# Emptying the seventh product's bank on ScalarE, and fixed places and a written order for the states of a state-space stage

## The chip, the core and the metric

The kernel runs on one core of a Trainium2 chip. The metric is the device time of one execution, in microseconds (us). Engines are named as in the profile: PE is TensorE (matmuls; PEld is its weight load, which overlaps), DVE is VectorE, ACT is ScalarE, POOL is GpSimd, SP is the queue that issues loads. ACT's queue issues the stores (ACTq in the profile's rows).

## The reference

One layer, model width 1024, sequence 1024, batch 1, float32. Two branches work on the same modulated input `h` and are merged by gates:

```python
proj = h @ w_in
gm_u, gm_v, gm_z, ssm_z, xbc, dt_raw, g_a, g_b = jnp.split(proj, SPLITS, axis=-1)
y_a = spatial_gating(gelu(gm_u), gelu(gm_v), ...) * silu(gm_z)          # 8 groups, chunks of 128
xbc = silu(causal_depthwise_conv(xbc, conv_w, conv_b))                  # 4 taps
xs, bm, cm = jnp.split(xbc, ...)
y_b = ssd_scan(xh, dt, a, bm, cm) + xh * d_skip[:, None]                # 8 groups of 4 heads of 64, state 128
y_b = rms_norm(y_b * silu(ssm_z), ssm_norm_w)                           # over each group
merged = sigmoid(g_a) * (y_a @ w_proj_a) + sigmoid(g_b) * (y_b @ w_proj_b)
out = rms_norm(x + gate * (merged @ w_out), final_norm_w)
```

`ssd_scan` works in chunks of 128. With the running sums `acs` of `dt*a` in a chunk, what a chunk gives is

```python
y_diag = (C_l . B_s) * exp(acs_l - acs_s) [l >= s] @ (x * dt)           # within the chunk
y_off  = (C_l @ state_before) * exp(acs_l)                              # from earlier chunks
state  = state * exp(acs_end) + B^T @ (x * dt * exp(acs_end - acs))     # handed on
```

## The kernel before

Every large product is kept at float32 precision by splitting both factors into a high and a low half (hi = rounded to `fp32r`, the type that PE takes; low = the rest), and adding three products: hi·hi, hi·lo, lo·hi. A rounding cast on ACT makes the high half, a subtraction on DVE the low one. The large products also use Strassen–Winograd: seven block products, `p1` to `p7`, in place of eight.

The order of work is partly written out. `pin` keeps an instruction in program order on its engine (all matmuls and transposes, by `mm` and `tp` at L81 and L84, and all loads, by `load` at L90); the rest is placed by a scheduler, which puts what stands under `high_priority` first. `later(n, f)` puts off a piece of work by n slots; a slot ends with `run_tasks`, after each product or item.

In the order in which PE comes to them:

1. Transposes, modulation and the first gate products (0 to some 70 us). `first_gate` ends with four `sg<-acc` activations on ACT (L473), each reading one PSUM bank.
2. The v block, `v_block` (L860 to L925): 28 units, each one of seven products at one of four `k`. A unit is 12 matmuls into four banks: `vx0` to `vx3`, or `vy0` to `vy3`. For each bank in turn come the three terms (`bh·wh`, `bl·wh`, `bh·wl`), `b` being the activations' halves and `w` the weights' (`p1v0h`, `p1v0l` for the first unit; the low half comes from DVE at L850).
3. The wide stage: pairs of output columns, `pair` (L540 to L598), of `cb`, `x`, `uz`, `z` and `g` columns, the number being the group. Each product is 12 matmuls (L536). `p1`, `p6`, `p7` and `p4` accumulate in one bank, `x…`; `p5` and `p3` in another, `y…`; `p2` in a third. After each product the bank is emptied by an operation under `high_priority`, recorded at L552: ACT copies for `p1`, `p5`, `p6` and `p4`, DVE adds for `p3`, `p2` and `p7`. The add after `p7` is `c2 = p5 + bank`; `p4`, which accumulates on in the same bank, is put off until after the next pair's `p5`, that is two products later. Beside it run the casts of the next pair's weights (L522 on ACT, L523 on DVE), the convolutions, and the splitting of the merged projections' weights (`wba`, `wbb`, `wbc`, from loads `wbr`; L787 on ACT, L792 on DVE, stored by `wb_d`).
4. The state-space stage, some 925 to 1146 us: a list of 32 steps, each a group and a pair of chunks, two groups alternating (`order`). `Group` holds the parts of a step:
   - `fetch`: two loads, `dcy` (running sums, broadcast) and `sl` (C, B, x and z of the two chunks), in a ring of 5 places.
   - `decay`: `ea` (ACT, L1063), the causal `affine_select` of `dcy` (POOL, L1066), eight exponentials on `dcy` (ACT, L1071).
   - `prep`: matmuls and transposes into the banks `pc` (C·B, and B transposed) and `px` (x transposed), then `xd` and `xe` (DVE, L1087), `dcy` times `pc` (DVE, L1091), and `bn`, the copy of B transposed (ACT, L1093).
   - `front`: eight matmuls into `yi` (within the chunks), the matmuls into `sp` (what each chunk adds to the state), and for each chunk a new state `st` in a ring of places: POOL multiplies the last state by its decay (L1119), DVE adds `sp` (L1121); the first one of a group is a DVE copy (L1117).
   - `back`: the matmuls into `yn` (from earlier chunks), then `evacuate`: `y` = d_skip·x + `yi` (DVE, L1147), `ym` = `yn`·`ea` (DVE, L1151), their sum (POOL, L1152), times z (POOL, L1153).
   - `post`: stores, then the squares (ACT, L1172, and a POOL add, L1173) put off by 5 slots, and the sums of squares later.

   Between these items `draw` puts in a few matmul pairs of `proj_a` (`pma`), the product with `w_proj_a`, which is independent of them. Its weights are split by `wa_block` at k = 1 of the block before: `wah` (ACT, L1276) and `wal` (DVE, L1277). For step n the list issues front(n), a draw, back(n), prep(n+2), fetch(n+6), decays(n+4).
5. The merged projections (L1548, 1146 to some 1330 us) and the output products (L1741, to the end).

Of the kernel before, what the change touches and what calls it, by code (L numbers as in the profile page):

```python
# [8 lines left out]
F32 = mybir.dt.float32  # L9
# [26 lines left out]
def hybrid_kernel(  # L36
# [505 lines left out]
    def pair(name, ops, done1, done2, after=None, whole=False):  # L542
# [7 lines left out]
        def out(f, *a):  # L550
            with tc.high_priority():
                keep(f(*a))  # L552
# [258 lines left out]
    def v_block():  # L811
# [94 lines left out]
        for u, (nm, k) in enumerate(units):  # L906
            _, bn, pn = V_OPS[u // 4]
            if u == 4:
                ps["y"] = [bank(f"vy{j}") for j in range(4)]
            for j in range(4):  # L910
                js = slice(j * P, (j + 1) * P)
                (bh, bl), (wh, wl) = (bop[bn][v][k] for v in range(2)), wops[u]
                for n, (l, r) in enumerate(((bh, wh), (bl, wh), (bh, wl))):
                    pin(PE.matmul(ps[pn][j], l[:, js], r, start=nm in ("p1", "p5", "p2") and n + k == 0,  # L914
                                  stop=n == 2 and k == 3, skip_group_check=nm not in ("p1", "p5", "p2")))
# [118 lines left out]
    nstep, nst = [0], [0]  # L1034

    class Group:

# [35 lines left out]
        def prep(self, s):  # L1073
            g, nm = self.g, f"{self.g}_{s}"
            sl, dcy, ea = self.pre[s]
            px, pc = bank(f"px{nm}"), bank(f"pc{nm}")
            for i in range(2):
                tsl = slice(i * P, (i + 1) * P)
                mm(pc[:, i * P : (i + 1) * P], sl[:, 1, tsl], sl[:, 0, tsl])
                tp(pc[:, 256 + i * P : 256 + (i + 1) * P], sl[:, 1, tsl], ident)  # L1080
                tp(px[:, i * 256 : i * 256 + P], sl[:, 2, tsl], ident)
                tp(px[:, i * 256 + P : i * 256 + 256], sl[:, 3, tsl], ident)
            x4 = px.rearrange("p (i h w) -> p i h w", i=2, h=HPG)
            xs = []
            for v, f in (("xd", dthq), ("xe", dde)):
                t = p2x.tile([P, 512], F32, name=f"{v}{nm}", tag=v, bufs=3)
                V.tensor_tensor(t.rearrange("p (i h w) -> p i h w", i=2, h=HPG), x4,  # L1087
                                fac(f, g, s).unsqueeze(3).to_broadcast([P, 2, HPG, HD]), op=ALU.mult)
                xs.append(t)
            d3 = dcy.rearrange("p h i l -> p h (i l)")  # L1090
            V.tensor_tensor(d3, d3, pc[:, 0:256].unsqueeze(1).to_broadcast([P, HPG, 256]), op=ALU.mult)  # L1091
            bn = p2x.tile([P, 256], F32, name=f"bn{nm}", tag="bn", bufs=3)
            A.copy(bn, pc[:, 256:512])  # L1093
            self.pre[s] = (sl, dcy, bn, xs[0], xs[1], ea)

        def front(self, s):
# [11 lines left out]
            self.y[s] = yi  # L1108
            self.sts = [self.st]
            for i in range(2 if s < NCH // 2 - 1 else 1):  # L1110
                mm(sp[:, i * 256 : (i + 1) * 256], bn[:, i * P : (i + 1) * P], xe[:, i * 256 : (i + 1) * 256])
            for i in range(2 if s < NCH // 2 - 1 else 1):
                pool, tag, b = st_r[nst[0] % 4 if nst[0] % 4 < 3 else 2]
                nst[0] += 1
                s2 = pool.tile([P, 512 if pool is hp else 256], F32, name=f"st{nm}_{i}", tag=tag, bufs=b)[:, 0:256]
                if self.st is None:
                    V.tensor_copy(s2, sp[:, 0:256])  # L1117
                else:
                    G.tensor_mul(v3(s2), v3(self.st),  # L1119
                                 fac(cd, g, s)[:, i].unsqueeze(2).to_broadcast([P, HPG, HD]))  # L1120
                    V.tensor_add(s2, s2, sp[:, i * 256 : (i + 1) * 256])  # L1121
                self.st = s2
                self.sts.append(s2)

        def back(self, s):

# [7 lines left out]
            self.evacuate(s, self.y.pop(s), yn)  # L1134
            if s % 2:
                self.post(s // 2)

        def evacuate(self, s, yi, yn):
# [6 lines left out]
            y1 = turn(y1_r, f"y1{nm}", F32).rearrange("p (j t) -> p j t", j=2)  # L1145
            for j in range(2):
                V.scalar_tensor_tensor(y1[:, j], sl[:, 2 + j], dskt[:, 2 * g + j : 2 * g + j + 1],  # L1147
                                       yi[:, j * 256 : (j + 1) * 256], op0=ALU.mult, op1=ALU.add)
            m = turn(ym_r, f"ym{nm}", F32).rearrange("p (j t) -> p j t", j=2)
            t0 = 0 if s else P  # L1150
            V.tensor_tensor(m[:, :, t0:], yn.rearrange("p (j l) -> p j l", j=2)[:, :, t0:], ea[:, :, t0:], op=ALU.mult)  # L1151
            G.tensor_add(y1[:, :, t0:], y1[:, :, t0:], m[:, :, t0:])  # L1152
            G.tensor_mul(yz, y1, sl[:, 4:6])  # L1153

        def post(self, q):

# [102 lines left out]
            pin(V.tensor_sub(yl[i], f32(yl[i]), f32(yh[i])))  # L1259
        yas.append((yh, yl))  # L1260

    war_r, wah_r, wal_r = [], [], []

    def wa_load(dd):
        war[dd] = []
# [6 lines left out]
    def wa_block(dd):  # L1272
        was[dd] = []
        for i, wr in enumerate(war.pop(dd)):
            wh, wl = turn(wah_r[0], f"wah{dd}_{i}"), turn(wal_r[0], f"wal{dd}_{i}")
            A.copy(wh, wr)  # L1276
            V.tensor_sub(wl, wr, f32(wh))  # L1277
            was[dd].append((wh, wl))

    def beside(n):  # L1280
# [74 lines left out]
    def proj_a():  # L1355

        for dd in range(KT):
# [8 lines left out]
            for k in range(KT):  # L1366
# [6 lines left out]
                    yield  # L1373
                if k == 1 and dd + 1 < KT:
                    wa_block(dd + 1)
            keep = pin if dd == KT - 1 else lambda i: i
            for h in range(2):
                keep(V.scalar_tensor_tensor(ths[h], ths[h], 1.0, pms[h], op0=ALU.add, op1=ALU.mult))
# [6 lines left out]
    st_r = [(hp, room.pop(0), 1), (p2x, "st", 1), (p2q, "st", 2)]  # L1385
    fetch(4)
    wa_load(1)
    fetch(5)
# [43 lines left out]
        run_tasks()  # L1432


    room.extend(ea_r[0] + [st_r[0][1]])
    room.extend(tag for k in range(KT - 2) for tag in ya_tags[k])
    draw(left[0] - 5)

# [439 lines left out]
```

## Time and profile before

| what | value |
|---|---|
| runs shown | 1401.98, 1403.64, 1404.79 us |
| median | 1403.64 us |
| the profiled execution | 1405.65 us, its span 1403.9 us, granted clock 0.995 |
| PE busy | 1371.6 us, 98% of the span, 6971 matmuls and transposes |
| DVE busy | 1053.8 us, 75% |
| ACT busy | 787.1 us, 56% |
| POOL busy | 212.4 us, 15%, most of it in the state-space stage |
| moved by DMA | 288.62 MB, 206 GB/s |

The profile records one execution: every instruction with its start, its length and what it waited for. A row of a view of waits reads: engine, what it works on, its line, then who released it; the total in us, how often, and the longest. A row of the timeline reads: start and length in us, engine, line, operation, out<-in, the shapes, and in brackets the idle time ahead of it with its releaser. A row of groups reads: line, engine, operation, shapes, count, then busy us and the mean length in ns, and the idle time ahead.

### The profile page before, as it was taken

What the parts mean: (1) busy time and instruction counts of PE and PEld (TensorE: products, weight loads), DVE (VectorE), ACT (ScalarE), POOL (GpSimd) and SP (SyncE); (2) the same over time, 40 slices, a digit from 0 to 9 for tenths busy, and PEclk for the clock granted to TensorE, in tenths of its full rate; (3) what the DMA queues carried; (4) which work ended last, traced back from release to release, by engine and by line L of the source; (5) the groups of instructions that cost most, each with busy time, mean ns of one, the idle gap of its engine ahead of it and who ended that gap; (6) DMA issues with size and microseconds to landing.
All of it is one profiled execution on the core that took longest, in us unless ns stands there. A gap on an engine that the chain in (4) does not pass through costs nothing.

```text
span 1403.9 us, 20510 instructions
## 1 busy us (share of the span) xinstructions
PE 1371.6 (98%) x6971; PEld 1134.5 (81%) x6971; DVE 1053.8 (75%) x1815; ACT 787.1 (56%) x1459; POOL 212.4 (15%) x208
## 2 busy tenths in 40 slices
PE   8999999999999999999999999999999999999997
PEld 7678888888888788787888888888888887888886
DVE  4777776687777889788888886388767765859976
ACT  5754656656656555455666555587766724223443
POOL 0000000000000011110100010027778750000001
PEclk9999999999999999999999999999999999999999
DMA  8675433343434777777665874498777758978913
GB/s 264 195 240 145 121 118 120 105 123 118 135 105 133 211 211 215 223 240 234 213 196 159 260 222 120 167 349 305 270 260 279 258 188 275 333 254 315 379 45 120
DMA packets 277182, 288.62 MB, mean 206 GB/s; under 512 B 15789, under 2 KB 224085, under 8 KB 277077
## 3 DMA queue, kind: packets, MB, share of 16 engines
q1 hardware_dynamic: 182420, 203.76, 45.8%
q10 hardware_dynamic: 94656, 83.54, 17.9%
q8 instruction: 55, 0.90, 0.3%
q14 instruction: 51, 0.41, 0.1%
HBM read 199.79 MB, written 87.46 MB: 205 GB/s over the span
## 4 chain that ended last, share of the span: by engine, by line
PE 67%; DMA 13%; DVE 9%; ACT 4%; issue 4%; POOL 2%; SPq 2%; ACTq 0%; DVEq 0%; POOLq 0%
PE xuz L536 6%; PE x L1548 6%; PE xcb L536 5%; PE yp L1548 5%; PE xx L536 4%; PE xz L536 4%; DMA wbr<-in_w_proj_b_dram 3%; PE vx L914 3%; PE xg L536 3%; PE yuz L536 3%; PE ycb L536 3%; PE pma L81 2%; PE ox L1741 2%; DMA dcy<-acs_d 2%; PE yx L536 2%
## 5 line engine op out<-in xcount | busy, mean ns | idle before, releaser
L755 POOL TENSOR_TENSOR wog<-wog,gb 128x256 f32<-128x256 f32 x16 | 16.7, 1062 | 625.1 <-DMA wog<-in_w_out_dram 625.1
L1071 ACT ACTIVATE dcy<-dcy,nacs 128x128 f32<-128x128 f32 x256 | 78.6, 389 | 14.7 <-POOL dcy L1066 14.2
L1066 POOL TENSOR_SCALAR_AFFINE_SELECT dcy<-dcy 128x1024 f32<-128x1024 f32 x32 | 35.0, 1093 | 136.8 <-ACT ea L1063 136.8
L986 ACT ACTIVATE ac<-ac 128x1024 f32<-128x1024 f32 x32 | 34.0, 1061 | 30.8 <-DVE ac L984 30.7
L1063 ACT ACTIVATE ea<-dcy 64x512 f32<-64x512 f32 x64 | 40.1, 626 | 13.0 <-DMA dcy<-acs_d 12.5
L81 PE MATMUL pma<-yh,wah 128*128 128x512 f32 x128 | 43.4, 420 | 0.0
L81 PE MATMUL pma<-yh,wal 128*128 128x512 f32 x128 | 42.6, 413 | 0.0
L1486 DVE SCALAR_TENSOR_TENSOR yn<-yn,par,rb 128x512 f32<-128x512 f32 x32 | 23.9, 748 | 24.6 <-DMA yn<-yb_d 24.6
L1091 DVE TENSOR_TENSOR dcy<-dcy,pc 128x1024 f32<-128x1024 f32 x32 | 38.9, 1217 | 4.4 <-PE pc L84 3.8
L1153 POOL TENSOR_TENSOR yz<-y,sl 128x512 f32<-128x512 f32 x32 | 41.4, 1293 | 1.1
L1151 DVE TENSOR_TENSOR ym<-yn,ea 128x512 f32<-128x512 f32 (+1 forms) x32 | 19.9, 623 | 28.5 <-PE yn L81 28.2
L81 PE MATMUL pma<-yl,wah 128*128 128x512 f32 x128 | 40.1, 394 | 0.0
L1152 POOL TENSOR_TENSOR y<-y,ym 128x512 f32<-128x512 f32 (+1 forms) x32 | 36.5, 1142 | 14.5 <-DVE ym L1151 13.7
L81 PEld LDWEIGHTS yn<-sl,st 128*128 128x128 f32 x224 | 30.2, 191 | 9.2 <-issue 2.9
L81 PE MATMUL yi<-dcy,xd 128*64 128x128 f32 x512 | 35.8, 283 | 1.8 <-DVE st L1121 1.8
L81 PE MATMUL yn<-sl,st 128*128 128x128 f32 x224 | 31.1, 276 | 6.0 <-DVE st L1121 6.0
L984 DVE SCALAR_TENSOR_TENSOR ac<-c2x,cwt,ac 128x1023 f32<-128x1023 f32 (+2 forms) x24 | 31.2, 1299 | 5.7 <-ACT ac L982 5.6
L81 PE MATMUL sp<-xe,bn 128*128 128x256 f32 x112 | 32.6, 408 | 2.7 <-DVE ssq L1182 1.5
L984 DVE SCALAR_TENSOR_TENSOR ac<-c2cb,cwt,ac 128x1023 f32<-128x1023 f32 (+2 forms) x24 | 31.1, 1294 | 4.4 <-ACT ac L982 4.3
L1119 POOL TENSOR_TENSOR st<-st,cd 128x256 f32<-128x256 f32 x48 | 32.9, 684 | 7.8 <-PE yn L81 5.5
L1756 POOL TENSOR_TENSOR r<-r,fnw 128x512 f32<-128x512 f32 x2 | 2.5, 1293 | 205.9 <-ACT junk L1754 205.9
L948 ACT ACTIVATE vm<-vm,vr 128x128 f32<-128x128 f32 x64 | 25.8, 484 | 14.0 <-DMA vm<-v_d 13.5
(2903 smaller groups left out, 4402.8 us busy)
## 6 DMA issues: line engine op xcount, KB each, us to landing
sl<-s_d SPq DMA_DIRECT2D x32, 768.0 KB
s_d<-ac ACTq DMA_DIRECT2D x32, 512.0 KB
dcy<-acs_d SPq DMA_DIRECT2D x32, 512.0 KB
av<-in_w_in_dram SPq DMA_DIRECT2D x36, 256.0 KB
aw<-in_ada_w_dram SPq DMA_DIRECT2D x16, 512.0 KB
wbr<-in_w_proj_b_dram SPq DMA_DIRECT2D x64, 128.0 KB
wb_d<-wbb ACTq DMA_DIRECT2D x32, 256.0 KB
wb_d<-wbc ACTq DMA_DIRECT2D x32, 256.0 KB
```

What stands on the lines that cost most here:

```text
L81: pin(PE.matmul(acc, l, r, start=first, stop=last))
L536: pin(PE.matmul(ps, lw[:, k * P : (k + 1) * P], r[k], start=first and n + k == 0, stop=n == 2 and k == 3, skip_group_check=not first))
L914: pin(PE.matmul(ps[pn][j], l[:, js], r, start=nm in ("p1", "p5", "p2") and n + k == 0, stop=n == 2 and k == 3, skip_group_check=nm not in ...
L984: V.scalar_tensor_tensor(ac[:, s:], cc[:, : S - s], conv_wt[:, 3 - s, i : i + 1], ac[:, s:], op0=ALU.mult, op1=ALU.add)
L986: A.activation(ac, ac, AF.Silu)
L1063: A.activation(ea[hh * HD : (hh + 1) * HD], dcy.rearrange("p (j e) i l -> p e j (i l)", e=2)[hh * HD : (hh + 1) * HD, hh], AF.Exp)
L1066: G.affine_select(out=d8, in_=d8, compare_op=ALU.is_ge, fill=-1e30, base=0, pattern=[[0, 2 * HPG], [1, P]], channel_multiplier=-1)
L1071: A.activation(dcy[:, h, i, :], dcy[:, h, i, :], AF.Exp, bias=sub[:, i, h : h + 1])
L1091: V.tensor_tensor(d3, d3, pc[:, 0:256].unsqueeze(1).to_broadcast([P, HPG, 256]), op=ALU.mult)
L1152: G.tensor_add(y1[:, :, t0:], y1[:, :, t0:], m[:, :, t0:])
L1153: G.tensor_mul(yz, y1, sl[:, 4:6])
L1548: pin(PE.matmul(ps[j], a[:, v, js], r, start=first and n + k == 0, stop=n == 2 and k == KT - 1, skip_group_check=not first))
```

## The change

Three parts of the kernel are edited.

In the wide stage's `pair` (not in the last pairs, those with the pool `p2r`), the bank of `p7` is copied by ACT into `c2`, under `high_priority`; the sum with `p5` is then a DVE add of two SBUF tiles, at the normal priority. In `v_block` the first two units go term by term over the four banks, in place of bank by bank.

In the state-space stage the states have fixed places: for each of the two alternating groups one for the state in the middle of a step (`mid`) and two for the one at its end, by turns. POOL's multiply for a step's first chunk moves from `front` into `back` of the step before. `y` = d_skip·x + `yi` moves from `evacuate` into `front`, between the two state adds. `prep` does the decay multiply first, then `bn`, then `xd` and `xe`; `bn` goes from ACT to DVE, and its ring from 3 to 2 places. All of these are pinned in program order (`prep` only from the third group or the second step on). The squares are put off by 8 slots in place of 5. The subtractions `wal` are collected in `lows` and issued at k = 3 and 4, pinned, in place of k = 1 (but for the first block).

By the two programs' instruction lists DVE has 33 instructions more after the change and PE, ACT, POOL and SP as many as before; 30 or so copies go from ACT to DVE, and as many from DVE's adds to ACT.

```diff
 pair()
-        out(V.tensor_add, c2[:, 512:1024], p5, px)
+        if p2r:
+            out(V.tensor_add, c2[:, 512:1024], p5, px)
+        else:
+            out(A.copy, c2[:, 512:1024], px)
+            V.tensor_add(c2[:, 512:1024], c2[:, 512:1024], p5)
 v_block()
-            for j in range(4):
+            (bh, bl), (wh, wl) = (bop[bn][v][k] for v in range(2)), wops[u]
+            terms = list(enumerate(((bh, wh), (bl, wh), (bh, wl))))
+            for j, (n, (l, r)) in [(j, t) for t in terms for j in range(4)] if u < 2 else [(j, t) for j in range(4) for t in terms]:
                 js = slice(j * P, (j + 1) * P)
...
 Group.prep()
+            keep = pin if s or g > 1 else lambda i: i
...
+            keep(V.tensor_tensor(d3, d3, pc[:, 0:256].unsqueeze(1).to_broadcast([P, HPG, 256]), op=ALU.mult))
+            bn = p2x.tile([P, 256], F32, name=f"bn{nm}", tag="bn", bufs=2)
+            keep(V.tensor_copy(bn, pc[:, 256:512]))
             for v, f in (("xd", dthq), ("xe", dde)):
...
-            A.copy(bn, pc[:, 256:512])
 Group.front()
+            last = s == NCH // 2 - 1
...
-                    G.tensor_mul(v3(s2), v3(self.st),
-                                 fac(cd, g, s)[:, i].unsqueeze(2).to_broadcast([P, HPG, HD]))
-                    V.tensor_add(s2, s2, sp[:, i * 256 : (i + 1) * 256])
...
+            mid, *ends = state(g % 2)
+            if s == 0:
+                pin(V.tensor_copy(mid, sp[:, 0:256]))
+            else:
+                pin(V.tensor_add(mid, mid, sp[:, 0:256]))
+            self.sts = [self.st, mid]
+            self.st = ends[s % 2]
+            if not last:
+                pin(G.tensor_mul(v3(self.st), v3(mid), fac(cd, g, s)[:, 1].unsqueeze(2).to_broadcast([P, HPG, HD])))
+            self.y1 = y1 = turn(y1_r, f"y1{nm}", F32).rearrange("p (j t) -> p j t", j=2)
+            for j in range(2):
+                pin(V.scalar_tensor_tensor(y1[:, j], sl[:, 2 + j], dskt[:, 2 * g + j : 2 * g + j + 1],
+                                           yi[:, j * 256 : (j + 1) * 256], op0=ALU.mult, op1=ALU.add))
+            if not last:
+                pin(V.tensor_add(self.st, self.st, sp[:, 256:512]))
 Group.back()
+            if s < NCH // 2 - 1:
+                mid = state(self.g % 2)[0].rearrange("p (h w) -> p h w", h=HPG)
+                pin(G.tensor_mul(mid, self.st.rearrange("p (h w) -> p h w", h=HPG),
+                                 fac(cd, self.g, s + 1)[:, 0].unsqueeze(2).to_broadcast([P, HPG, HD])))
...
 Group.evacuate()
+            pin(V.tensor_tensor(m[:, :, t0:], yn..., ea[:, :, t0:], op=ALU.mult))
+            pin(G.tensor_add(y1[:, :, t0:], y1[:, :, t0:], m[:, :, t0:]))
+            pin(G.tensor_mul(yz, y1, sl[:, 4:6]))
 Group.post()
-                later(5, self.squares, yz, [yz[:, j] for j in range(2)])
+                later(8, self.squares, yz, [yz[:, j] for j in range(2)])
 wa_block()
-            V.tensor_sub(wl, wr, f32(wh))
+            if dd == 0:
+                V.tensor_sub(wl, wr, f32(wh))
+            else:
+                lows.append((wl, wr, wh))
 proj_a()
                 if k == 1 and dd + 1 < KT:
                     wa_block(dd + 1)
+                elif k in (3, 4) and lows:
+                    wl, wr, wh = lows.pop(0)
+                    pin(V.tensor_sub(wl, wr, f32(wh)))
...
+    st2 = hp.tile([P, 512], F32, name="st2", tag=st_tag)
+    sts = [st2[:, 0:256], st2[:, 256:512]]
+    sts += [pool.tile([P, 256], F32, name=f"st{n}", tag="st", bufs=2) for pool in (p2x, p2q) for n in range(2)]
+
+    def state(n):
+        return sts[n], sts[2 + n], sts[4 + n]
```

More of the change, by code (lines that the diff above doesn't have):

```diff
@@ L909, in v_block @@
                 ps["y"] = [bank(f"vy{j}") for j in range(4)]
-            for j in range(4):
+            (bh, bl), (wh, wl) = (bop[bn][v][k] for v in range(2)), wops[u]
+            terms = list(enumerate(((bh, wh), (bl, wh), (bh, wl))))
+            for j, (n, (l, r)) in [(j, t) for t in terms for j in range(4)] if u < 2 else [(j, t) for j in range(4) for t in terms]:
                 js = slice(j * P, (j + 1) * P)
[L912 to L915, printed above, removed]
+                pin(PE.matmul(ps[pn][j], l[:, js], r, start=nm in ("p1", "p5", "p2") and n + k == 0,
+                              stop=n == 2 and k == 3, skip_group_check=nm not in ("p1", "p5", "p2")))
             wops.pop(u)
@@ L1033, in hybrid_kernel @@
     NSET = 5
-    nstep, nst = [0], [0]
+    nstep = [0]
     class Group:
@@ L1107, in front @@
             sp = bank(f"sp{nm}")
-            self.y[s] = yi
-            self.sts = [self.st]
-            for i in range(2 if s < NCH // 2 - 1 else 1):
+            last = s == NCH // 2 - 1
+            for i in range(1 if last else 2):
                 mm(sp[:, i * 256 : (i + 1) * 256], bn[:, i * P : (i + 1) * P], xe[:, i * 256 : (i + 1) * 256])
[L1112 to L1119, printed above, removed]
-                                 fac(cd, g, s)[:, i].unsqueeze(2).to_broadcast([P, HPG, HD]))
-                    V.tensor_add(s2, s2, sp[:, i * 256 : (i + 1) * 256])
-                self.st = s2
-                self.sts.append(s2)
+            mid, *ends = state(g % 2)
[13 more added lines that the diff above has]
+                pin(V.tensor_add(self.st, self.st, sp[:, 256:512]))
         def back(self, s):
@@ L1144, in evacuate @@
             yz = self.yz[s // 2][:, :, (s % 2) * 256 : (s % 2 + 1) * 256]
[L1145 to L1148, printed above, removed]
             m = turn(ym_r, f"ym{nm}", F32).rearrange("p (j t) -> p j t", j=2)
             t0 = 0 if s else P
-            V.tensor_tensor(m[:, :, t0:], yn.rearrange("p (j l) -> p j l", j=2)[:, :, t0:], ea[:, :, t0:], op=ALU.mult)
-            G.tensor_add(y1[:, :, t0:], y1[:, :, t0:], m[:, :, t0:])
-            G.tensor_mul(yz, y1, sl[:, 4:6])
+            pin(V.tensor_tensor(m[:, :, t0:], yn.rearrange("p (j l) -> p j l", j=2)[:, :, t0:], ea[:, :, t0:], op=ALU.mult))
+            pin(G.tensor_add(y1[:, :, t0:], y1[:, :, t0:], m[:, :, t0:]))
+            pin(G.tensor_mul(yz, y1, sl[:, 4:6]))
         def post(self, q):
@@ L1260, in ya_operand @@
         yas.append((yh, yl))
-    war_r, wah_r, wal_r = [], [], []
+    war_r, wah_r, wal_r, lows = [], [], [], []
     def wa_load(dd):
```

16 lines of the change are left out of this document (7 added, 9 removed).

## The prediction

> **What bounds the kernel now.** I read the page first, for who is busy; then the waits of TensorE, for what its idle time is owed to; then the stretches of the state-space stage; then the timeline around each wait that the change touches.
>
> ```profile
> PE 1371.6 (98%) x6971; PEld 1134.5 (81%) x6971; DVE 1053.8 (75%) x1815; ACT 787.1 (56%) x1459; POOL 212.4 (15%) x208
> ```
>
> TensorE (PE) sets the time. The change takes no matmul away (6971 stay), so it can only win what PE waits for, and lose by making PE wait more. The waits of PE (us in total, times, longest):
>
> ```profile
> PE yn L81 <- DVE st L1121: 6.0, 4, 2.4
> ...
> PE xuz L536 <- DVE c2uz L552: 1.9, 1, 1.9
> PE yi L81 <- DVE st L1121: 1.8, 1, 1.8
> PE sp L81 <- DVE ssq L1182: 1.5, 1, 1.5
> PE xz L536 <- DVE c2z L552: 1.4, 2, 1.1
> PE sp L81 <- DVE xe L1087: 1.2, 2, 0.6
> PE x L1548 <- DVE tha L1378: 1.2, 1, 1.2
> PE vx L914 <- DVE p1v0l L850: 1.2, 1, 1.2
> PE xcb L536 <- DVE c2cb L552: 1.0, 1, 1.0
> PE xx L536 <- DVE c2x L552: 0.5, 1, 0.5
> PE pc L81 <- ACT bn L1093: 0.4, 1, 0.4
> ```
>
> Three groups lie under the edits. The wide stage: 1.9 + 1.4 + 1.0 + 0.5 = 4.8 us, each the fourth product of a pair waiting until VectorE (DVE) has emptied the bank of the seventh. The state-space stage: 6.0 + 1.8 + 1.5 + 1.2 + 0.4 = 10.9. The first v product: 1.2. Together 16.9 us is all there is to win, 1.2% of the 1403.64. The wait on `tha` belongs to the merged projections and stays.
>
> The state-space sum can be cross-checked from the stretches (us, busy time of PE, PEld, DVE, ACT, POOL, with instruction counts, PE clock, DMA share, GB/s):
>
> ```profile
> 950.00:1000.00 50.00, 49.37 (x382) 43.08 (x381) 39.36 (x71) 38.29 (x102) 39.62 (x40) 1.00 0.84 298
> ...
> sum 200.00, PE 189.07 PEld 165.21 DVE 144.17 ACT 129.24 POOL 156.38; mean PE 47.27 PEld 41.30 DVE 36.04 ACT 32.31 POOL 39.09
> ```
>
> The second row is 950 to 1150: PE idles 200 − 189.07 = 10.9. No other engine is full: DVE 72%, POOL 78%. So the waits come from order and latency, not from load.
>
> **The v block's order.** The start of the first product:
>
> ```profile
> 71.95 0.62 ACT L473 ACTIVATE sg<-acc 128x512 f32<-128x512 f32 x1
> ...
> 72.25 0.50 PE L914 MATMUL vx<-p1v0l,b11h 128*128 128x512 f32 x1 [1.15 <-DVE p1v0l L850]
> ```
>
> Before, the third matmul needs the low half `p1v0l`, and waits from 72.25 − 1.15 = 71.10. Now the low half is first needed by the ninth, so that wait goes. But the fourth matmul now goes to the fourth bank, `vx3`, and by the program's allocation that bank is the one that the fourth gate activation above still reads until 71.95 + 0.62 = 72.57. So PE stands again after one matmul more, and goes on at 72.57 with nine matmuls left, where before it went on at 72.25 with ten. So the product ends 0.32 later less one matmul, which takes the 0.50 of the row or, without the restart in it, less: between −0.2 and +0.3, and I take **+0.1**. If that bank is free after all, −1.2; so the bounds are −1.2 and +0.3.
>
> **The copy of the seventh product.** It removes a DVE add from the path and puts there a ScalarE (ACT) copy; the add stays on DVE, on two SBUF tiles, behind nothing that PE needs soon (the buffer `p5` it frees is wanted by the next pair's copy, whose bank is next written two products later).
>
> ```profile
> 471.54 0.61 ACT L522 CAST p4cb4h<-a22cb 128x512 fp32r<-128x512 f32 x1
> ...
> 474.36 0.59 ACT L552 COPY c1cb<-xcb 128x512 f32<-128x512 f32 x1 [0.35 <-issue]
> 474.40 0.68 DVE L552 TENSOR_TENSOR c2uz<-p5uz,xuz 128x512 f32<-128x512 f32 x1
> ...
> 572.92 0.37 ACTq L93 DMA_DIRECT2D wb_d<-wbb  x1
> ...
> 573.61 0.68 DVE L552 TENSOR_TENSOR c2z<-p5z,xz 128x512 f32<-128x512 f32 x1
> ...
> 613.43 0.30 ACT L787 CAST wba<-wbr 128x128 fp32r<-128x128 f32 x1 [1.50 <-DMA wbr<-in_w_proj_b_dram]
> ```
>
> A copy of that shape costs 0.59. ACT is 56% busy, so 31 copies (18 us) fit. What counts is where ACT stands. For `uz` (the longest wait) ACT is free after its cast at 472.15; the copy ends at 472.74, where the add ended at 475.08, and PE's wait began about 475.08 − 1.9 = 473.2: the whole 1.9 goes. For `z` ACT issues a store until 573.29; the copy ends at 573.88, the add at 574.29: only 0.4 of it goes. For the other three (`cb`, the second `z`, `x`) ACT's queue gives the same picture and I take 0.5 each. Sum −1.9 − 0.4 − 1.5 = −3.8. Against it a new wait: at 613.43 ACT has stood 1.50 for a DMA with its casts, and the copy of that moment's pair would be queued behind. I take +0.9 of the 1.50. Sum **−2.9**. Bounds: the best is all, −4.8; the worst is that ACT is no earlier than DVE except at `uz`, and three such DMA waits instead of one: −1.9 + 2.7 = +0.8.
>
> That the copy can't step past the waiting cast is seen in the row at 613.43. The Trainium skill, PSUM — Partial Sum Buffer, "Engine vs sequencer instructions", gives it as a rule that speaks against this edit: the queues of ScalarE, VectorE and GpSimd are strict FIFO. By it the 0.9 stands; without it this part would give −3.8.
>
> **The state-space stage.**
>
> ```profile
> 1026.30 0.75 DVE L1277 TENSOR_TENSOR wal<-wa,wah 128x512 fp32r<-128x512 f32 x1 [2.04 <-ACT wah L1276]
> ...
> 1107.14 1.09 POOL L1066 TENSOR_SCALAR_AFFINE_SELECT dcy<-dcy 128x1024 f32<-128x1024 f32 x1 [3.12 <-ACT ea L1063]
> ...
> 1108.84 0.42 DVE L1121 TENSOR_TENSOR st<-st,sp 128x256 f32<-128x256 f32 x1 [4.66 <-POOL st L1119]
> ```
>
> These are the two causes. The low half `wal` sits in DVE's queue ahead of the state add and waits for ACT's cast; PE's `yn` waits for that state (three of the four long waits, some 6 us). And the state add waits for POOL's multiply, which stands behind the affine select, which waits for ACT: that is the 1.8 of `yi`. After the change `wal` is issued two to three k later, that is 6 to 9 of `proj_a`'s matmul pairs, more than the 4 or 5 of one step, so it meets a cast that is done. The first state add of a step no longer waits in its own front: its multiply was issued in the step before. The copy of `bn`, on which `pc` waited 0.4, leaves ACT's queue. What POOL waits for ACT in this stage:
>
> ```profile
> POOL dcy L1066 <- ACT ea L1063: 23.7, 18, 3.1
> ```
>
> So 6.0 + 1.8 + 0.4 = 8.2 goes. What is late next is the bank that `sp` reuses: it is the `px` bank, freed by `xe`, the 1.5 + 1.2 that stay (the row that names `ssq` is the same bank, with `ssq` in the queue ahead). `bn` now precedes `xd` and `xe` on DVE:
>
> ```profile
> L1117 DVE COPY st<-sp 128x256 f32<-128x256 f32 x6 | 2.5, 419 | 0.9 <-PE sp L81 0.9
> ...
> L1153 POOL TENSOR_TENSOR yz<-y,sl 128x512 f32<-128x512 f32 x32 | 41.4, 1293 | 1.1
> ```
>
> A DVE copy of that shape out of PSUM takes 0.42, so the banks come free up to 0.42 later; at the three places where PE waits for them that is 3 × 0.42 = 1.3, less the state add (0.42) that no longer stands there, at one or two of them: +0.7. Elsewhere the cover is DVE's slack: 30 copies × 0.42 = 12.6 us on DVE. In the fullest stretch, 950 to 1000, DVE idles 10.6 us; with about 8 steps in it (32 steps in some 205 us) that is 1.3 us a step, and 0.9 is left. Sum −8.2 + 0.7 = **−7.5**. Bounds: everything goes, also the `sp` waits, −10.9; or POOL's lag brings half of the 8.2 back and the banks cost the full 1.3: −4.1 + 1.3, about −3.
>
> The squares' later due slot and the order of `xd`, `xe` after the decay multiply move work within POOL's and DVE's slack; I cost them at nothing, and the next rival is what they cost if that slack is gone.
>
> **Sum.** +0.1 − 2.9 − 7.5 = −10.3. The profiled execution was 1405.65, all but 1.75 of it its span, so 1395.4 for a run like it. It lies 2.0 above the median of the runs shown, 1403.64; from the median the forecast is 1393.3.
>
> **Rivals.**
> *Slower: POOL's lag, pinned into DVE.* The second state add of a step is pinned on DVE ahead of `ym` and of the next preparation, and waits for POOL's second multiply in its front. POOL's queue may hold `yz` (1.29 by L1153) and an affine that waits for ACT (23.7/18 = 1.3) ahead of that multiply. Then 24 steps (all but the last of each group) lose 1.29 + 1.3 less DVE's slack, 1.1 (between the 0.9 and the 1.3 above), = 1.5 each: 36 us, a time of 1393.3 + 36 = 1429. It decides once POOL lags by more than that slack in most steps; a lag in a third of them would eat the gain. For: POOL 78% busy and the wait of 4.66 above. Against: POOL had 22% idle, the first multiply moves out of the front, and the squares are put off. By the FIFO rule of the Trainium skill named above nothing could overtake the affine; the wait of 3.12 agrees.
>
> *The stage's gain is eaten upstream.* The loads of decays and sequences wait for POOL's last read of a buffer:
>
> ```profile
> SPq L90 <- POOL yz L1153: 103.1, 26, 8.9
> ```
>
> If PE, running faster, meets that ring, the 7.5 is lost: −2.8, a time of 1400.8.
>
> *All waits go.* 1403.6 − 16.9 = 1386.7; with 1.7 for the spread of the runs shown (1403.64 − 1401.98), 1385. Against it speak the bank that `sp` reuses, which the change frees later, and the rows at 71.95 and 613.43.
>
> *The edits of the two early stages do nothing:* ACT as late as DVE except at `uz` (−1.9 + 0.9) and v at +0.1: 1403.6 − 0.9 − 7.5 = 1395.2. The store's issue at 572.92 speaks for it, the end of the cast at 472.15 against.
>
> **How the numbers follow.** Forecast around 1393 (1387 to 1398): 0.55. Early edits idle: 0.08. Ring: 0.15, a third of it within 0.2% of before. All waits gone: 0.08. Slower: 0.14. 0.2%, about what a measurement of this kernel can tell from no change, is 2.8 us. Faster 0.55 + 0.08 + 0.10 + 0.08 = 0.81, same 0.05, slower 0.14. The range runs from 1385, all waits gone and the spread below, to the ring's 1400.8 with 1.2 for that spread (1404.79 − 1403.64): 1402. It leaves out the slower rival and the ends of the others, about 0.2.
>
> **What would show it.** In the profile after: the rows `yn <- st` and `yi <- st` of PE's waits gone or under 2 us together; no `wal <- wah` wait on DVE above 1 us; `sp <- xe` waits of 2.5 to 4 us; the `c2` rows replaced by waits on ACT's `c2`, under 2 us in all, one of them near 614; a wait of `vx` for `sg` near 71.2. Wrong if DVE's `st <- POOL st` grows beyond 20 us with PE waiting behind it (the slower rival), if PE waits for `dcy` or `yi` on ACT (the ring), or if PE's idle time from 950 to 1150 stays above 8 us.

## The result and the profile after

| kernel | runs | median us | lowest to highest |
|---|---|---|---|
| before | 5 | 1401.98 | 1400.51 to 1404.79 |
| changed | 5 | 1408.48 | 1406.65 to 1409.26 |

The change makes the kernel slower: ratio 1.0043, 95% interval 1.0025 to 1.006, or 6 us (3.5 to 8.4). The forecast was 1393.3, the range 1385 to 1402. The profiled execution after has a span of 1407.5 us. Here and below the ratio is the one on record with the run; it is not the quotient of the two medians, from which it differs by up to 0.11%. Disturbed runs are left out everywhere (two of the twelve of e9).

What PE waits for after the change (same view as in the prediction: us in total, times, longest):

```profile
PE yp L84 <- POOL ssq L1193: 5.0, 2, 3.7
PE pp L84 <- DMA pk<-in_ada_b_dram: 3.5, 1, 3.5
PE sp L81 <- DVE ym L1158: 3.1, 2, 1.6
PE sp L81 <- DVE ssq L1189: 2.9, 3, 1.0
PE yn L81 <- DVE st L1120: 2.6, 4, 1.8
PE xz L536 <- ACT c2z L552: 2.0, 2, 1.2
PE xg L536 <- ACT c2g L552: 1.9, 2, 1.2
PE px L84 <- DVE x L379: 1.4, 1, 1.4
PE sp L81 <- DVE st L1130: 1.3, 2, 0.8
PE vx L918 <- ACT sg L473: 1.3, 1, 1.3
```

Every wait that was to go has gone or shrunk: `yn` for `st` from 6.0 to 2.6, `yi` for `st` and `pc` for `bn` to nothing, `vx` for the low half, and the waits of `uz`, `cb` and `x` pairs on DVE's `c2`. In their place stand `sp` (2.7 before, 3.1 + 2.9 + 1.3 = 7.3 now), `yi` for others (further down in the same view: 0.9 for ACT's exponentials, 0.7 with no releaser shown, 0.2 for POOL, together the 1.8 that it was before), `z` and `g` pairs on ACT's `c2`, the gate activation, and one that was not there at all: 5.0 us of `yp` for the power of the sums of squares, in the merged projections, which the change does not touch. The idle time of PE from 950 to 1150 is what it was, 200 − 188.39 = 11.6 against 10.9:

```profile
sum 200.00, PE 188.39 PEld 164.40 DVE 153.87 ACT 119.00 POOL 154.98; mean PE 47.10 PEld 41.10 DVE 38.47 ACT 29.75 POOL 38.74
```

To see where time went I cut each trace at the starts of five matmuls: the first of the v block, of the wide stage, of `proj_a`, of the merged projections, and the last of all. The table (us between those starts) has the two kernels and the experiments told below. "Old" and "new" say which code the stage has; the order in the last stage is the scheduler's.

| profile of | wide stage | state-space stage | the rest |
|---|---|---|---|
| before | 776.2 old | 236.0 old | 234.5 |
| changed | 772.3 new | 235.6 new | 240.2 |
| e1 | 776.9 new | 237.5 old | 236.5 |
| e2 | 771.5 old | 237.2 new | 239.0 |
| e3 | 775.4 new | 236.3 new | 233.5 |
| e4 | 774.7 new | 235.5 repaired | 233.5 |
| e5 | 775.8 new | 236.3 old | 234.3 |
| e6 | 769.8 old | 233.9 old | 236.7 |
| e7 | 778.8 six pairs new | 235.6 old | 234.6 |
| e8 | 771.3 old | 232.4 repaired | 236.9 |
| e9 | 773.6 old | 234.8 new | 233.1 |
| e10 | 772.4 old | 233.9 new, less POOL work | 233.0 |
| e11 | 773.9 old | 241.4 new, `xd` and `xe` first | 234.6 |
| e12 | 770.8 old | 231.1 repaired twice | 234.8 |

The v block took 77.61 to 77.67 in the profiles with the old order and 77.74 to 77.78 with the new one.

One profile each is little. What the table's spread is made of can be had from the same traces, by adding up the idle time ahead of PE's instructions between those starts. In the wide stage PE was idle for 1.3 to 5.2 us in the eight profiles of the old code (mean 3.5) and 4.2 to 6.9 in the five of the new (mean 5.9). In the state-space stage it was 9.0 to 11.0 in five profiles of the old code and 8.6 to 12.1 in four of the new (means 10.2 and 10.1), 8.3 (e4) and 7.5 (e8) in two of the repaired, 6.4 in e12 and 15.0 in e11. Up to the first matmul of `proj_a`, DVE, ACT and POOL have the same instructions in the same order in all eight profiles with the old wide stage, so what differs there is the execution and not the program (but for the v block's matmuls in e6).

### The profile page after: what moved, and what is told of

The parts are those of the page before. It is cut to its first block, busy times and chain, and to the rows that moved or that the text cites. A ratio compares the mean times of both kernels' runs of the same rounds, so it can differ in the third digit from the quotient of the medians.

```text
span 1407.5 us, 20602 instructions
## 1 busy us (share of the span) xinstructions
PE 1370.2 (97%) x6971; PEld 1134.7 (81%) x6971; DVE 1065.4 (76%) x1847; ACT 794.8 (56%) x1464; POOL 214.0 (15%) x208
## 4 chain that ended last, share of the span: by engine, by line
PE 68%; DMA 13%; DVE 8%; ACT 3%; issue 3%; POOL 2%; SPq 2%; ACTq 0%; DVEq 0%; POOLq 0%
PE xuz L536 6%; PE xx L536 6%; PE xcb L536 5%; PE xz L536 4%; PE xg L536 3%; DMA dcy<-acs_d 3%; PE vx L918 3%; PE yuz L536 3%; PE yp L1568 3%; PE x L1568 3%; PE yx L536 3%; PE pma L81 3%; PE ycb L536 3%; PE ox L1761 2%; DMA wbr<-in_w_proj_b_dram 2%
## 5 line engine op out<-in xcount | busy, mean ns | idle before, releaser
L1130 DVE TENSOR_TENSOR st<-st,sp 128x256 f32<-128x256 f32 x24 | 10.1, 420 | 31.6 <-POOL st L1124 31.4
L988 DVE SCALAR_TENSOR_TENSOR ac<-c1cb,cwt,ac 128x1023 f32<-128x1023 f32 (+2 forms) x24 | 31.6, 1317 | 1.3 <-ACT ac L986 1.3
## 6 DMA issues: line engine op xcount, KB each, us to landing
sl<-s_d SPq DMA_DIRECT2D x32, 768.0 KB
```

Source lines behind the costliest of these rows:

```text
L988: V.scalar_tensor_tensor(ac[:, s:], cc[:, : S - s], conv_wt[:, 3 - s, i : i + 1], ac[:, s:], op0=ALU.mult, op1=ALU.add)
```

## The experiments

Each was timed beside the kernel before, on the same chip.

### e1, e5, e6, e7: the two early edits

e1 is the kernel before with both early edits; e5 has the copy alone, e6 the v block's order alone, and e7 the copy in six pairs only:

```diff
-        if p2r:
+        if name not in ("uz7", "z1", "cb5", "x5", "g6", "x6"):
             out(V.tensor_add, c2[:, 512:1024], p5, px)
```

> The kernel before with only the two early edits (the seventh product's copy and the v block's order). Theory A (from the two profiles, the early stages gained about 2.4 us, the state-space stage nothing, and the merged projections lost 5): about 2.4 us faster than before, 1399.6. Rival (the early gain is a matter of where the half-clock windows fell in the one profile): within 1 us of before. The v block alone: a wait of 1.3 us on the gate activation in place of one of 1.2 on the low half, so 0 within 0.2.

> The kernel before with the copy of the seventh product alone. Theory Q (ACT's queue: the copy waits behind ACT's own waits in other pairs): new waits of PE on ACT's c2 at two or more g and z pairs, about 1 us each, as large in sum as the DVE waits that go; 1401 to 1404. Rival (the loss of the two early edits together came from the v block): 2 to 5 us faster than before, 1398 to 1400.

> The kernel before with the v block's order alone. Theory (one wait for another): the wait on the gate activation is 1.3 in place of 1.2 on the low half, the block ends 0.1 to 0.5 later, 1402 to 1403; PE's wait for c1uz near 185 stays at 0.3 to 0.5. Rival (the order shifts the transfers after the block): that wait is 2 us, with a stretch at half clock behind it, and the time is 3 to 4 longer than before.

> The kernel before with the copy of the seventh product in six pairs alone, those where PE waited for DVE's add before (uz7, z1, cb5, x5, g6, x6). Theory Q: the waits on c2 all but go, without the new ones, and so does the stretch at half clock behind the longest; 4 to 7 us faster than before, 1396 to 1398. Rival (waits move on whatever is done there): within 2 us of before.

| kernel | median us | before, same job | ratio, 95% interval |
|---|---|---|---|
| e1, both | 1406.85 | 1402.56 | 1.0025 (1.0012 to 1.0038) |
| e5, copy | 1406.86 | 1404.05 | 1.0026 (1.001 to 1.0043) |
| e6, v block | 1402.26 | 1404.05 | 0.9998 (0.998 to 1.0016) |
| e7, copy in six pairs | 1409.55 | 1404.05 | 1.0042 (1.0023 to 1.0061) |

The v block costs nothing that shows (and `c1uz` waits 0.4 in e6, so its rival falls), and the copy costs 0.26%, 3.7 us (1.4 to 6.0). e1 is 3.5 us slower than before and so missed both of its expectations. e5 is slower than theory Q's 1401 to 1404, but its waits of PE show Q's new waits on ACT:

```profile
PE xz L536 <- ACT c2z L552: 2.6, 3, 1.0
...
PE xuz L536 <- ACT c1uz L552: 1.8, 1, 1.8
PE xg L536 <- ACT c2g L552: 1.8, 2, 1.4
```

The longest on `c2`, 1.4, is in the pair where the prediction placed one (`g4`, near 614). The timeline of e5, ACT and PE:

```profile
614.85 0.30 ACT L791 CAST wba<-wbr 128x128 fp32r<-128x128 f32 x1 [1.94 <-DMA wbr<-in_w_proj_b_dram]
...
615.05 0.61 ACT L522 CAST p4z2h<-a22z 128x512 fp32r<-128x512 f32 x1
...
615.58 0.58 ACT L552 COPY c2g<-xg 128x512 f32<-128x512 f32 x1
...
616.20 1.20 PE L536 MATMUL xg<-t4h,p4g4h 128*128 128x512 f32 x4 [1.41 <-ACT c2g L552]
```

ACT stands 1.94 for a load; two casts and then the copy are queued behind, and PE, which was done with the product before, waits 1.41.

The other half of the loss is that there was less to win than one profile said. e6 has the old code in the wide stage, and its waits there are

```profile
PE xg L536 <- DVE c2g L552: 0.5, 1, 0.5
PE xuz L536 <- ACT c1uz L552: 0.4, 1, 0.4
...
PE xx L536 <- DVE c2x L552: 0.2, 1, 0.2
```

against 4.8 us on DVE's `c2` in the profile of before: the 1.9 of `uz` is not there. In the profile of before DVE had stood 3.60 for the load `ag` ten us ahead of that wait; in e6's, with the same operations in between, 1.83. e6 is the lowest of the eight profiles with the old code: on DVE's `c2` PE waited 0.7 to 4.8 us in them, 2.9 in the mean, and the prediction read the highest. By the table, the old wide stage took 769.8 to 773.9 in the seven others and 776.2 in the one that the prediction read; the new one 772.3 to 776.9. So a part of those waits belongs to the code, and a good part to how that one execution's loads fell. In the five profiles of the new code PE waits 3.1 to 4.4 us on `c2` (mean 4.0): the copy moved those waits and won nothing.

e7 refutes both theories of its expectation, by its time. Its six pairs are not quite those that waited, though: in the profile of before they were `uz7`, `z1`, `cb5`, `z2` and `x5`. `z2` (1.1) is not in e7's list, and `g6` and `x6` had no wait there. And PE waited more for DVE in pairs that the edit leaves alone:

```profile
PE xz L536 <- DVE c2z L552: 5.4, 3, 2.4
```

The three are `z0` 1.4, `z2` 1.7 and `z4` 2.4. The longest can be followed: in e7's trace the weights' sum `s1cb`, which stood 2.07 for the load `a22cb` at 766, is ahead of the add into `c1z` on DVE, and DVE works without a pause from there to `c2z`, late by that wait; in e6's trace, with the order of the kernel before, that add comes first. So the scheduler placed DVE's unpinned work of this stage anew around the edit. Why the two others grew is not settled.

Not settled either: 1.8 of e5's waits are `c1uz`, one copy behind ACT's activations of `vm`, whose load lands some 1.5 us later than before (counted from the start of the wide stage). It was 1.8 to 2.3 in four of the five profiles with the copy in the early pairs, and 0.2 to 0.6 in the fifth and in all with the old code there. In the mean of the profiles PE's waits on ACT's `c1` grew by 1.4 us, on `c2` by 1.1: this open wait is the larger part of what the copy cost.

### e2, e3, e9: the state-space part, and an order far behind it

e2 is the changed kernel without the early edits. e3 is the changed kernel, and e9 is e2, with the last two sums-of-squares operations held in their old place on DVE:

```diff
-            V.tensor_scalar(ssq[...], pq[:, 0:4], 1.0 / 256, EPS, ...)
+            (pin if g >= NG - 2 and q == 1 else lambda i: i)(V.tensor_scalar(ssq[...], ...))
 y_norm()
-        V.scalar_tensor_tensor(t, t, snw[...], rbs[n // 2, h], ...)
+        (pin if n >= KT and h == 1 else lambda i: i)(V.scalar_tensor_tensor(t, t, ...))
```

> The changed kernel without the two early edits: only the state-space stage is changed. Theory A: 2.4 us slower than the changed kernel, 1410.9, that is 9 slower than before; the two waits of PE on the power of the sums of squares (5 us in the changed kernel's profile) are there again. Rival (the early edits are the loss): 1405 or less.

> The changed kernel with one order put back in the merged projections: the last two sums-of-squares operations on DVE are held ahead of the first normalisation of the second half, where the kernel before had them. Theory A (the scheduler moved them behind a normalisation that waits for its load, and PE waits for them): the two waits on the power, 5.0 us, go, and the time falls by 5 to 1403.5. Rival (the load is what is late, and the wait only turns into one on the next operand): within 1.5 us of the changed kernel's 1408.5.

> The kernel before with the state-space part alone and the order in the merged projections held as before; the second multiply stays on POOL, as in the change. It splits the 7.6 us between the state-space part alone and the same with both repairs. Theory A+P: the order is worth 4 and the multiply 3.5, so this is at 1403 to 1404, level with before. Rival: the multiply did it all, and this stays at 1406 to 1408.

| kernel | median us | before, same job | ratio, 95% interval |
|---|---|---|---|
| e2, state-space part | 1407.58 | 1402.56 | 1.0036 (1.0023 to 1.005) |
| e3, whole change, order held | 1405.01 | 1402.56 | 1.0012 (0.9998 to 1.0026) |
| e9, state-space part, order held | 1403.86 | 1404.27 | 1.0005 (0.999 to 1.002) |

Holding the order is worth 0.31% with the early edits (1.0043 to 1.0012) and 0.31% without (1.0036 to 1.0005): 4.4 us, with some 3 to either side by the two intervals of each difference. e9 is level with before, so the state-space part brings nothing that shows (2 us to either side), and the moved order is most of the loss. (e2's own expectation put the loss at 9; it was 5, since the early edits lose too.) DVE's rows show it. Before:

```profile
1169.01 0.16 DVE L1182 TENSOR_SCALAR ssq<-yp 128x4 f32<-128x4 f32 x1
1172.81 0.75 DVE L1486 SCALAR_TENSOR_TENSOR yn<-yn,par,rb 128x512 f32<-128x512 f32 x1 [3.64 <-DMA yn<-yb_d]
```

After, on DVE and then on PE:

```profile
1170.96 0.75 DVE L1506 SCALAR_TENSOR_TENSOR yn<-yn,par,rb 128x512 f32<-128x512 f32 x1 [3.16 <-DMA yn<-yb_d]
1171.63 0.68 DVE L1544 TENSOR_TENSOR p1bl<-yn,p1bh 128x512 fp32r<-128x512 f32 x1
1172.23 0.15 DVE L1189 TENSOR_SCALAR ssq<-yp 128x4 f32<-128x4 f32 x1
...
1178.28 0.75 DVE L1506 SCALAR_TENSOR_TENSOR yn<-yn,par,rb 128x512 f32<-128x512 f32 x1 [2.02 <-DMA yn<-yb_d]
1178.94 0.15 DVE L1189 TENSOR_SCALAR ssq<-yp 128x4 f32<-128x4 f32 x1
...
1174.16 0.27 PE L84 MATMUL yp<-ident,ssq 128*8 128x128 f32 x1 [1.27 <-POOL ssq L1193]
...
1180.88 0.27 PE L84 MATMUL yp<-ident,ssq 128*8 128x128 f32 x1 [3.68 <-POOL ssq L1193]
```

The operation takes 0.15 us. Before, it stood ahead of a normalisation that waits 3.64 for its load; after, behind it. The second of the two, at 1178.94, likewise stands behind a normalisation that waits 2.02, and PE's longer wait, 3.68, is for the power (1.65 on POOL) of that one. No line of this code was edited: the scheduler, given another state-space stage, ordered DVE's unpinned work differently some 30 us later. The wait on POOL's power is 5.0 in the changed kernel and 4.0 in e2, the two with the moved order, and is in no other profile; with the order held, in e3 and e9, it is gone.

### e4, e8, e10, e11: why the state-space stage gained nothing

e4 is e3, and e8 is e9, with the state's second multiply on DVE. e10 is e9 without POOL's addition of squares, so that half of each group's squares is missing from the norm. e11 is e9 with `xd` and `xe` first:

```diff
 e4, e8: front()
-                pin(G.tensor_mul(v3(self.st), v3(mid), fac(cd, g, s)[:, 1]...))
+                pin(V.tensor_mul(v3(self.st), v3(mid), fac(cd, g, s)[:, 1]...))
 e10: squares()
-            G.tensor_add(sq[0], sq[0], sq[1])
 e11: prep()
-            keep(V.tensor_tensor(d3, d3, pc[:, 0:256]..., op=ALU.mult))
-            keep(V.tensor_copy(bn, pc[:, 256:512]))
             for v, f in (("xd", dthq), ("xe", dde)):
                 ...
+            keep(V.tensor_tensor(d3, d3, pc[:, 0:256]..., op=ALU.mult))
+            keep(V.tensor_copy(bn, pc[:, 256:512]))
```

> As the run before, and the state's second multiply in each step (24 of them) goes from POOL to DVE, so that DVE's second add has no POOL to wait for. Theory P (DVE, pinned, stands for POOL's lag, and so frees the banks late): the 31 us of that wait go, PE's waits for sp, 7 us, fall under 3, and the time is 4 to 6 us under the run before. Rival L (DVE's load and the place of the copy of B transposed ahead of xd and xe): DVE gets 24 x 0.7 = 17 us more, PE's waits for sp stay or grow, and the time is the same or up to 4 us longer.

> The kernel before with the state-space part alone, the order in the merged projections held as before, and the second multiply on DVE. Theory P: no wait of DVE for POOL's state multiply; the waits that remain on PE in the state-space stage are 3 to 7 us, 1395 to 1399. Rival R (with that wait gone the load ring is what is late): one or two waits of 2 to 5 us for sp or yi, with ACT's first exponential waiting for its load ahead of them, and 1400 to 1403.

> As the run before, but POOL's addition of the two squares is left out (half of each group's squares is missing from the norm): POOL has 14 x 1.27 = 18 us less in its queue. Theory P (POOL's lag, through the pinned add): DVE's wait for POOL's state multiply falls to under half, PE's waits for sp fall by 3 or more, and the time is 3 to 6 under the run before. Rival L (DVE's own load and order): DVE's wait may fall, but PE's waits and the time stay within 1.5.

> As e9, but xd and xe come ahead of the decay multiply and the copy of B transposed on DVE, still pinned. Rival L (xe last frees the bank late): the bank of px is free 1.5 us earlier in each step, PE's waits for sp fall by 4 or more, and the time by 3 to 5. Theory P: DVE is late as a whole, only the waits under 1.5 us go, 1 to 2 us.

| kernel | median us | before, same job | ratio, 95% interval |
|---|---|---|---|
| e4 | 1401.51 | 1402.56 | 0.9987 (0.9975 to 0.9999) |
| e8 | 1399.96 | 1404.05 | 0.9979 (0.9962 to 0.9996) |
| e10 | 1400.49 | 1404.27 | 0.9979 (0.9963 to 0.9994) |
| e11 | 1407.19 | 1404.27 | 1.002 (1.0006 to 1.0035) |

The multiply on DVE is worth 0.25% (e4 against e3) and 0.26% (e8 against e9), 3.6 us with some 3 to either side, though it gives DVE 24 instructions more: DVE's load was not what bound the stage. What held it is in the rows from 940 to 1190, of the kernel before and of the changed one:

```profile
DVE st L1121 <- POOL st L1119: 12.2, 8, 4.7
DVE st L1130 <- POOL st L1124: 31.0, 17, 3.5
```

12.2 before (both adds of a step), 31.0 now for the second alone: that pinned add waits for POOL in 17 of 24 steps. One of them, on POOL, then DVE, then PE:

```profile
1013.50 1.64 POOL L1193 TENSOR_TENSOR ssq<-ssq,nhalf 128x8 f32<-128x8 f32 x1
1016.11 1.27 POOL L1180 TENSOR_TENSOR yz<-yz 128x512 f32<-128x512 f32 x1 [0.97 <-ACT yz L1179]
1017.34 0.61 POOL L1124 TENSOR_TENSOR st<-st,cd 128x256 f32<-128x256 f32 x1
...
1017.98 0.42 DVE L1130 TENSOR_TENSOR st<-st,sp 128x256 f32<-128x256 f32 x1 [3.45 <-POOL st L1124]
1018.32 0.68 DVE L1158 TENSOR_TENSOR ym<-yn,ea 128x512 f32<-128x512 f32 x1
...
1019.06 1.13 PE L81 MATMUL sp<-xe,bn 128*128 128x256 f32 x4 [1.56 <-DVE ym L1158]
```

POOL's multiply of 0.61 stands behind a power (1.64) and the squares' addition (1.27 after a wait of 0.97 for ACT). DVE, with nothing free to go ahead, stands 3.45; `ym`, pinned behind the add, ends late, and PE's `sp` waits 1.56 for it, though its operands are there (the last `xe` ended at 1013.4): by that it waits for a bank.

e11 speaks against rival L by its time: with `xe` earlier the kernel is slower than the one before, which e9 is not, and L had it 3 to 5 us faster than e9. But it does not refute L's mechanism. PE's waits for `sp` did fall, from 6.6 in e9 to 4.1; those for `yi`, `yn` and `tha` grew from 1.9 to 10.8, among them 1.5 of `yi` for the decay multiply that now comes behind `xd` and `xe`. So the order that frees the bank sooner makes others wait, and what L's bank alone is worth stays open. Theory P's 1 to 2 us did not come either. e10 speaks for P by its time, 0.26% under e9, but not by its waits: DVE's wait for POOL's multiply fell only from 27.7 to 22.2 and PE's waits for `sp` from 6.6 to 6.4. So it does not tell what of its gain came from POOL's queue. Open as well is what part of the lag comes from operations that are slow beside each other: in the changed kernel the subtractions `wal` at 1025.42 and 1030.93, while POOL works, take 1.22 and 1.60, where most take 0.68. No run separates that.

With the multiply on DVE, e8 has rival R's long wait instead. PE, DVE and ACT:

```profile
1095.35 2.04 PE L81 MATMUL sp<-xe,bn 128*128 128x256 f32 x4 [4.51 <-DVE ssq L1186]
...
1092.46 1.22 DVE L1087 TENSOR_TENSOR dcy<-dcy,pc 128x1024 f32<-128x1024 f32 x1 [3.03 <-POOL yz L1156]
...
1088.63 1.27 ACT L1063 ACTIVATE ea<-dcy 64x512 f32<-64x512 f32 x2 [2.05 <-DMA dcy<-acs_d]
1089.92 2.74 ACT L1071 ACTIVATE dcy<-dcy,nacs 128x128 f32<-128x128 f32 x9
```

DVE's decay multiply waits for eight exponentials, the last of which ends about when POOL does (the profile names POOL). ACT was idle before them for 2.05, because the next step's `ea` stands ahead of them in its queue and waits for a load. That load had been issued by SP right after POOL's `yz` let the buffer go:

```profile
1081.57 1.27 POOL L1156 TENSOR_TENSOR yz<-y,sl 128x512 f32<-128x512 f32 x1
...
1083.29 0.38 SPq L90 DMA_DIRECT2D dcy<-acs_d  x1
```

So theory P's expectation held in part. DVE's wait for POOL's state multiply is gone from both, and PE's idle time in the stage fell from 9.7 (e3) to 8.3 (e4) and from 8.6 (e9) to 7.5 (e8). But PE's waits for `sp` did not fall below 3: they are 6.9 in e4 as in e3, and 6.4 in e8 against 6.6, of which this one wait is 5.0 and 4.5.

### e12: the ring shortened

e12 is e8 with POOL's multiply for the next step's first chunk put behind `evacuate` in `back`, so that POOL's last read of the step's buffers comes 0.6 us sooner:

```diff
 back()
+            self.evacuate(s, self.y1, yn)
             if s < NCH // 2 - 1:
                 ...
                 pin(G.tensor_mul(mid, ...))
-            self.evacuate(s, self.y1, yn)
```

> The state-space part with both repairs, and POOL's multiply for the next step's first chunk moved behind POOL's last read of the step's buffers. Theory R (the load ring is what is late once DVE no longer waits: POOL's last read, the load, ACT's first exponential, which stands ahead of the exponentials of the step before, then DVE and the bank): the loads go out 0.6 earlier, the one long wait of PE for sp (4.5 us) shrinks by 0.6 or more and with it the time by 1 to 3, to 1397 to 1399. Rival: the wait stays within 0.3 of 4.5, and the time within 1 of 1400.

1400.27 us beside 1404.27, ratio 0.9968 (0.9951 to 0.9986): by its ratio the fastest kernel here, 4.5 us faster than before (2.0 to 6.9). Its waits for `sp` are

```profile
PE sp L81 <- DVE ssq L1186: 4.9, 3, 3.0
```

where e8's were 6.4, the longest 4.5. Theory R expected the longest to shrink by 0.6 or more; it shrank by 1.5, in the same step. The time is within 1 us of 1400, as the rival had it, and the gain over e8 by the ratios (0.9979 to 0.9968) is within their intervals: the wait is shown, its worth in time is not.

## Why the prediction was wrong, point by point

- **What bounds the kernel** held: PE's waits decide, and no matmul went. But "16.9 us is all there is to win" took one execution's waits for the code's. For the wide stage that was wrong (4.8 us on DVE's `c2` in that profile, 2.9 in the mean of eight). For the state-space stage it was right in sum (PE idle 9.0 to 11.0 in five profiles; `yn` on `st` 4.9 to 5.4 in the four later ones with the old code), but the 1.8 of `yi` was 0 to 1.9 there. It also left out the half clock behind two of the waits, told at the end.
- **The v block**, +0.1: right, and by the steps given: PE waits 1.3 for the gate activation ahead of the fourth matmul, and the block is 0.1 to 0.2 longer.
- **The copy**, −2.9: measured +3.7. The step that failed is the sum of gains, −3.8, since those waits come and go with the loads and new ones of the same size took their place. The mechanism of the cost was right (the queue behind a wait for a load, at the `g4` pair), but it was counted once at 0.9; after the change four pairs wait on ACT, 2.0 + 1.9 in all. The 1.8 to 2.3 of `c1uz` in four profiles was not in the sum at all. The bound for the worst, +0.8, was too narrow as well. Two small readings were off: 37 copies went to ACT, not 31 (78 of `c2` in the changed kernel's trace, 41 before; 32 of `bn` went the other way, so ACT has five instructions more by the two profiles), and the 0.4 for `z1` is more than the 0.3 that PE waited there.
- **The state-space stage**, −7.5: measured 0 (e9, 0.05% with 0.15% to either side). What the edits were aimed at did go: `wal`'s waits for `wah` fell from 8.2 us to one of 2.0, and of the 8.2 on PE 2.6 was left under the same names. Two terms failed. The 1.8 of `yi` came back in full for other releasers. And "what is late next", put at +0.7 for banks freed 0.42 later, was 7.3 − 2.7 = 4.6 on `sp` alone. The reason that the runs show is the first rival's mechanism, POOL's lag pinned into DVE; its mark (more than 20 us of `st` for POOL) was met at 31.0, and taking POOL out of that chain brought 3.6 us. Its price of 36 us was wrong: DVE's wait grew by 19, but PE's waits for `sp` by 4.6 only; in the rows at 1017.98 and 1019.06 DVE stood 3.45 and PE 1.56. PE's idle time from 950 to 1150, 11.6, is the prediction's other sign of being wrong (above 8).
- **The ring** rival was right about the place. In the changed kernel its sign, `yi` waiting for ACT, is there with 0.9 only; with DVE's wait for POOL gone (e8) it cost 4.5 us in one wait, and not the whole gain.
- **Not in the prediction at all**: the 4.4 us of the moved order. The two instruction lists, which can be compared without a run, show both sums one normalisation further back. I compared the stages that the diff touches and not what lies behind them.

By the single experiments the parts are 0 (v block) + 3.7 (copy) + 0.7 (state-space stage) + 4.4 (order) = 8.8 us, and the whole is 6 (3.5 to 8.4); their intervals, 2 to 3 us each, cover the difference.

## What to carry to other kernels

Before a wait of one or two microseconds is booked as a gain, ask whether it belongs to the code or to how loads fell in that execution; more profiles of the same code answer it. Where a scheduler orders unpinned work, compare the whole instruction lists on every engine to the end, for an edit can move a short operation behind a load far from its lines. And pinning an order hands the waits of the slowest engine in the chain to all that is queued behind: here moving one short multiply off the lagging engine turned a stage that gained nothing into a gain of 2.9 us (e8), and of 4.5 with a buffer's last reader let go first (e12), though these two cannot be told apart.

## What the runs showed of the hardware

A wait of PE can be followed by 3.41 us at half clock (from 475.5 to 478.9 in the profile of before), so that it costs some 1.7 us (half of that) more than its length. In the profile of before, the stretch behind the wait of `uz` and the one after it (us, busy time of PE, PEld, DVE, ACT, POOL, with instruction counts, then PE's granted clock, DMA share, GB/s):

```profile
475.50:478.50 3.00, 3.00 (x9) 2.32 (x8) 3.00 (x7) 0.45 (x1) 0.00 (x0) 0.50 0.33 87
479.00:482.00 3.00, 3.00 (x15) 2.44 (x14) 2.06 (x8) 2.80 (x5) 0.00 (x0) 1.00 0.72 189
```

In 3 us, 9 matmuls ran at half clock and 15 at full. Behind the 3.68 of `yp` in the changed kernel the clock was 0.55 from 1182 to 1185. Between the start-up and the last products the 14 traces have 30 such stretches, of 3.41 us or, four times, of twice that. All seven waits of PE above 2.7 us had one, 7 of the 10 between 2.0 and 2.7, and about one in three of those from 1.5 to 2.0; a few came with waits of 1.0 to 1.5, and two with no wait above 0.5, which is not explained. PE's idle time, and 1.7 for each 3.41 us at half clock, account for the wide stage's spread: without them it is 768.0 to 769.3 us in all 14. The Trainium skill, TensorE: Matmul & The Clock Gate, "HAM oscillation — how this bites in real kernels", gives as the abstract rule no idle gaps above about 3.4 us; here waits of 1.9 us (`uz`) to 3.0 us were followed by it too, and the measurement decides. The prediction counted the waits of `uz` (1.9) and `yn` (2.4) without it.
